# Layer 0's input projection of a two-layer decoder kernel: pairs of column tiles by Strassen's seven products, and mixer outputs kept in DRAM

## The chip, the cores and the metric

The kernel runs on one core of a Trainium2 chip. The metric is the device time of one execution in microseconds (us); of several runs the median is given. Engines are named as in the profile: PE is TensorE's matrix multiplication, PEld its weight loads, DVE is VectorE, ACT is ScalarE, POOL is GpSimd, SP is the engine that issues the DMA transfers here. "L183" is line 183 of the kernel whose trace is read.

## The reference

x has 1024 tokens (SEQ) of 1024 channels (D_MODEL), in float32. Two layers follow each other, then a last RMSNorm. Layer 0, where the change is, computes

```python
def rms_norm(x, g):
    r = x32 * lax.rsqrt(jnp.mean(x32 * x32, axis=-1, keepdims=True) + NORM_EPS)
    return (r * g.astype(jnp.float32)).astype(x.dtype)

def even_mixer(y, w_in, w_pool, pool_scale, conv_w, w_out):
    proj = y @ w_in                       # 1024 x 1024 by 1024 x 6144
    u_a, gate_b, gate_c, h_c, z = jnp.split(proj, [...], axis=-1)
    pooled = causal_multiscale_pool(...)  # trailing means over 2, 4, 8, 16 tokens, minus u_a
    a = jnp.einsum("bsgc,gcd->bsgd", pooled, w_pool).reshape(b, s, POOL_WIDTH) * pool_scale
    cu = gate_c * h_c
    v = conv_w[2] * cu + conv_w[1] * shift_right(cu, 1) + conv_w[0] * shift_right(cu, 2)
    bo = gate_b * v
    out = jnp.concatenate([a, bo], axis=-1) * jax.nn.silu(z)
    return out @ w_out
```

with y the normalized x. Layer 1 is a sliding-window attention with its own projections. The result is 1024 x 1024 in float32.

## The kernel before

**Tiles.** Channels lie on the 128 partitions, tokens along the row, in two halves (HALF) of 512. A column tile of w_in is 128 output channels: 8 contraction tiles of 128x128. w_in has 48 of them: u_a 0 to 7, gate_b 8 to 15, gate_c 16 to 23, h_c 24 to 31, z 32 to 47. Float32 accuracy comes from splitting each operand into a high and a low part (`split`: ACT casts the high part, L175, DVE subtracts it, L176): a product is three matmuls, high·high, high·low and low·high (`mm3`, L182 to L184), each with a 128x128 stationary tile and 512 columns. A column tile costs 8 x 3 matmuls for each half of the tokens (`proj_half`, `proj`).

**The start.** x comes in 16 tiles of 128x512 (`load_x`, L356). ACT multiplies each by g1 into uH (L359), DVE makes the low part uL (L360); no division by the root mean square is made at this point. So the matmuls of the first two column tiles (L411 to L413) take each contraction tile as it arrives. Meanwhile ACT squares x and DVE and POOL add the squares up (L369); column sums by the tensor engine and a Newton iteration (`rsqrt_mean`, L136 to L145) give r for each token, which is spread over all partitions by two matmuls on a diagonal matrix (`diag_r`, L156, and `spread_r`). r enters when a bank of PSUM is emptied, as a factor r_b (L442, L456).

**Order.** TensorE's instructions stand in the order of the program. Those of ACT, DVE and SP stand in program order only in the start (`order()`); from there on a scheduler places them, and an engine takes its instructions strictly in the order placed. Weights are loaded into a pool W of 9 buffers; `take()` splits one unit ahead and loads three ahead. PSUM has banks psA and psD (two each) and psB (four).

**The groups.** Four pooling groups follow (u_a tiles 2g and 2g+1, gates 32+2g and 33+2g, windows 2, 4, 8, 16; the sums over a window are L465 rows of about 1024 columns, and a mixing product with w_pool of 24 matmuls, `mix`), then eight convolution groups (tiles 16+j, 24+j, 40+j, 8+j). The mixer's outputs `o`, 16 x 2 tiles of 128x512, stay in SBUF. The output projection (L564 to L566) takes them, split by `operands(s)`, with w_out. After it comes layer 1.

**Small work.** The rotary tables (`rope_tables`, L203 and further, on DVE) and `small_loads` (the positions posi, the bias bkv and the attention sinks, with nsink on DVE, L248) are placed among the first groups.

## Time and profile before

| | |
|---|---|
| median of three runs | 1156.97 us (1155.9 to 1157.88) |
| span of the profiled execution, its own time from first to last instruction | 1158.2 us |
| PE busy | 1126.6 us, 5248 matmuls |
| DVE, ACT, POOL busy | 619.2, 386.6, 272.6 us |
| mean granted clock of PE | 0.992 |
| bytes moved | 83.92 MB, 72 GB/s over the span |

The span is what the rows of the trace add up to; it is 1.2 us above the median of the other runs. A clock of 1.00 is TensorE's level of 2.4 GHz, 0.5 that of 1.2 GHz. In rows, "x8" is a count of instructions that are run together, "[0.79 <-DVE U L360]" an idle time of the engine just ahead of the row and what ended it.

### The profile page before, as it was taken

The page shows a single profiled execution, that of the slowest core. Times are in us where ns is not written, and L with a number is a line of the kernel's source. Part 1 is how long each engine was busy: PE and PEld are TensorE (multiplying, and loading weights), DVE is VectorE, ACT ScalarE, POOL GpSimd, SP SyncE. Part 2 cuts the span into 40 slices and gives each one's busy share as a digit, 9 for nine tenths or more (in the row PEclk, how much of TensorE's full clock was granted, in tenths as well). Part 3 has the DMA queues.
Part 4 walks back from the last instruction along what each step waited for, and adds up shares of the span by engine and source line. Part 5 has one row for each costly group of instructions (what it writes and reads, how often), then busy time and mean ns, then how long its engine had stood idle before and what let it go on. Part 6 is the DMA issues. An engine that isn't in the chain of part 4 may idle for free.

```text
span 1158.2 us, 14036 instructions
## 1 busy us (share of the span) xinstructions
PE 1126.6 (97%) x5248; PEld 921.5 (80%) x5248; DVE 619.2 (53%) x1109; ACT 386.6 (33%) x797; POOL 272.6 (24%) x427
## 2 busy tenths in 40 slices
PE   9999999999999999999999999999999998898897
PEld 6788888888888888888888788898888886677676
DVE  7993637332233223223655865641133669899995
ACT  8132122111111111111432532420012687776653
POOL 1200000010010110110101100143330036787874
PEclk9899999999999999999999999999999999999999
DMA  7111111111111111111144344520022405460001
GB/s 242 45 47 55 46 52 49 55 41 51 55 37 55 55 37 55 54 38 64 59 148 148 110 164 144 177 80 1 19 69 95 146 19 120 64 90 21 19 19 55
DMA packets 59892, 83.92 MB, mean 72 GB/s; under 512 B 36272, under 2 KB 37424, under 8 KB 59824
## 3 DMA queue, kind: packets, MB, share of 16 engines
q1 hardware_dynamic: 59824, 83.03, 23.4%
q8 instruction: 41, 0.67, 0.2%
q14 instruction: 27, 0.22, 0.1%
HBM read 74.63 MB, written 8.39 MB: 72 GB/s over the span
## 4 chain that ended last, share of the span: by engine, by line
PE 85%; DVE 8%; ACT 3%; issue 1%; DMA 1%; SPq 1%; POOL 0%; ACTq 0%; DVEq 0%
PE psB L184 8%; PE psB L183 8%; PE psB L182 8%; PE psA L184 5%; PE psA L183 5%; PE psA L182 5%; PE psD L184 5%; PE psD L183 5%; PE psD L182 5%; PE psA L566 2%; PE psA L564 2%; PE psA L565 2%; PE psD L566 2%; PE psD L564 2%; PE psD L565 2%
## 5 line engine op out<-in xcount | busy, mean ns | idle before, releaser
L175 ACT CAST W<-W 128x1024 fp32r<-128x1024 f32 (+2 forms) x109 | 107.4, 988 | 531.7 <-DVE W L176 427.0
L176 DVE TENSOR_TENSOR W<-W 128x1024 fp32r<-128x1024 f32 (+2 forms) x109 | 125.4, 1155 | 235.6 <-PE psB L183 177.8
L183 PE MATMUL psB<-U,W 128*128 128x512 f32 x384 | 152.6, 397 | 2.0 <-DVE U L360 1.8
L184 PE MATMUL psB<-U,W 128*128 128x512 f32 x384 | 152.7, 398 | 0.0
L182 PE MATMUL psB<-U,W 128*128 128x512 f32 x384 | 150.7, 392 | 0.0
L183 PEld LDWEIGHTS psB<-U,W 128*128 128x128 f32 x384 | 72.9, 190 | 20.8 <-DVE U L360 4.0
L521 POOL TENSOR_TENSOR T<-T,r_b 128x1024 f32<-128x1024 f32 x8 | 19.3, 2416 | 290.6 <-DVE T L519 290.6
L182 PEld LDWEIGHTS psB<-U,W 128*128 128x128 f32 x384 | 72.9, 190 | 16.4
L184 PEld LDWEIGHTS psB<-U,W 128*128 128x128 f32 x384 | 73.1, 190 | 14.5
L184 PE MATMUL psD<-U,W 128*128 128x512 f32 x184 | 72.5, 394 | 0.0
L184 PE MATMUL psA<-U,W 128*128 128x512 f32 x184 | 72.5, 394 | 0.0
L183 PE MATMUL psD<-U,W 128*128 128x512 f32 x184 | 72.2, 392 | 0.0
L183 PE MATMUL psA<-U,W 128*128 128x512 f32 x184 | 72.1, 392 | 0.0
L182 PE MATMUL psA<-U,W 128*128 128x512 f32 x184 | 71.5, 389 | 0.0
L182 PE MATMUL psD<-U,W 128*128 128x512 f32 x184 | 71.4, 388 | 0.0
L582 POOL TENSOR_TENSOR t<-t,T 128x512 f32<-128x512 f32 x14 | 19.2, 1370 | 170.5 <-ACT T L581 170.5
L734 ACT ACTIVATE pt<-psB,smax 128x128 f32<-128x128 f32 x128 | 45.5, 367 | 25.0 <-DVE smax L731 21.6
L722 PE MATMUL psB<-kT,qT 128*128 128x256 f32 (+1 forms) x128 | 35.2, 297 | 17.3 <-ACT qT L703 9.4
L875 PE MATMUL psD<-O,aH 128*128 128x512 f32 (+1 forms) x128 | 51.1, 399 | 0.0
L566 PE MATMUL psA<-U,W 128*128 128x512 f32 x128 | 50.4, 394 | 0.5 <-DVE W L176 0.5
L566 PE MATMUL psD<-U,W 128*128 128x512 f32 x128 | 50.3, 393 | 0.0
L564 PE MATMUL psD<-U,W 128*128 128x512 f32 x128 | 50.1, 392 | 0.0
(291 smaller groups left out, 2588.0 us busy)
## 6 DMA issues: line engine op xcount, KB each, us to landing
W<-w_in SPq DMA_DIRECT2D x46, 512.0 KB, 3.5
W<-w_out SPq DMA_DIRECT2D x32, 512.0 KB, 3.7
W<-w_z SPq DMA_DIRECT2D x16, 512.0 KB, 3.4
O<-xT SPq DMA_DIRECT2D x16, 256.0 KB, 5.0
T<-xT SPq DMA_DIRECT2D x16, 256.0 KB, 4.2
h_dram<-T SPq DMA_DIRECT2D x16, 256.0 KB, 2.2
W<-w_q SPq DMA_DIRECT2D x8, 512.0 KB, 4.3
U<-h_dram SPq DMA_DIRECT2D x8, 512.0 KB, 5.7
```

The lines of the kernel that those rows point to most:

```text
L175: nc.scalar.copy(out=dst_h, in_=src)
L176: sub(out=dst_l, in0=src, in1=dst_h.bitcast(F32), op=ALU.subtract)
L182: mm(dst, lhsT=ah, rhs=bh, start=(i == 0), stop=False)
L183: mm(dst, lhsT=ah, rhs=bl, start=False, stop=False)
L184: mm(dst, lhsT=al, rhs=bh, start=False, stop=(i == n - 1))
L521: ptt(out=v[:, 0:S], in0=v[:, 0:S], in1=r_b, op=ALU.mult)
L564: mm(dst, lhsT=w[k][0], rhs=oHL[f][0], start=(f == 0), stop=False)
L565: mm(dst, lhsT=w[k][0], rhs=oHL[f][1], start=False, stop=False)
L566: mm(dst, lhsT=w[k][1], rhs=oHL[f][0], start=False, stop=(f == 15))
L722: mm(dst, lhsT=lq, rhs=kT[:, 2 * g, lo:(b + 1) * P], start=True, stop=False)
L734: exps.append(act(out=res[g][:, 2 * i2 + i, :], in_=bv[:, i, P:256], func=AF.Exp, scale=0.125, bias=smax[:, at + i:at + i + 1], accum_out= ...
L875: mm(o, lhsT=a[0][:, kk, :], rhs=woH[8 * n + k][:, c], start=(k == 0), stop=False)
```

## The change

Two column tiles of w_in, 256 output channels, are taken as a matrix of 2 x 2 blocks A (rows: the two column tiles; columns: the two halves of the contraction), and the normalized x as 2 x 2 blocks B (rows: halves of the contraction; columns: halves of the tokens). A block product has four contraction tiles. Instead of eight block products there are seven, of sums of blocks: A11·B11, A12·B21, S1·T1, S2·T2, S3·T3, S4·B22 and A22·T4, where S1 = A21 + A22, S2 = S1 - A11, S3 = A11 - A21, S4 = A12 - S2 and T1 = B12 - B11, T2 = B22 - T1, T3 = B22 - B12, T4 = T2 - B21 up to sign. The sums of weights are made on POOL for each pair (four of 128x512), the sums of x once at the start. Each product is 4 x 3 matmuls (`product`); the partial sums of a pair are combined when its banks are emptied (`pair`: L417, L422, L426, L429, L431 of the new kernel on DVE, a copy L405 on ACT). Three of the seven continue in a bank from which a partial sum has been read, with start=False. LEAD says how many products ahead weights are prepared.

Since the blocks of x are combined across token halves, x is normalized before the first product (`stats`, `normed`, L476, `operand`). The first four products are A11 and A12 of pairs 0 and 1. `spill` writes each finished output to o_dram, and `operands` loads it again. The output projection and layer 1 are the same code.

```diff
...
+    order_ = ("A11", "S2", "A12", "S3", "S1", "A22", "S4")
+    prods = [(0, "A11"), (0, "A12"), (1, "A11"), (1, "A12")]
+    prods += [(i, n) for i in range(2) for n in order_ if n not in ("A11", "A12")]
+    prods += [(i, n) for i in range(2, len(pairs)) for n in order_]
...
+            if what == "S2":
+                wsum[i] = s1 = bp.tile([P, 4, P], F32, name="S1", bufs=2)
+                ptt(out=s1, in0=a21, in1=a22, op=ALU.add)
+                ptt(out=a21, in0=a11, in1=a21, op=ALU.subtract)
+                ptt(out=a11, in0=s1, in1=a11, op=ALU.subtract)
+            if what == "S3":
+                ptt(out=a12, in0=a12, in1=a11, op=ALU.subtract)
...
+            hl = W([P, 2, 4, P], F32R)
+            split(hl[:, 0], hl[:, 1], src)
...
+    def product(dst, i, what, b, start=True):
+
+        prepare_to(at[i, what] + 1 + LEAD)
+        w, x = whl[i, what], ops[b]
+        for k in range(4):
+            for n, (hw, hx) in enumerate(((0, 0), (0, 1), (1, 0))):
+                mm(dst, lhsT=w[:, hw, k], rhs=x[hx][k], start=start and k + n == 0,
+                   stop=k == 3 and n == 2, skip_group_check=not start)
...
+    def pair(i, outs, c11=None, first=None):
+
+        b1, p1 = first or first_products(i)
+        b2 = bank(2)
+        product(b2, i, "S2", "T2")
+        u2_ = t2()
+        tt(out=u2_, in0=b2, in1=p1, op=ALU.add)
+        if first is None:
+            second_products(i, b1)
+            c11(b1)
+        product(b2, i, "S3", "T3", False)
+        tt(out=p1, in0=b2, in1=p1, op=ALU.add)
+        b3 = bank(3)
+        product(b3, i, "S1", "T1")
+        o12, o21, o22 = outs
+        tt(out=o22, in0=b3, in1=p1, op=ALU.add)
+        b4 = bank(4)
+        product(b4, i, "A22", "T4")
+        tt(out=o21, in0=b4, in1=p1, op=ALU.add)
+        product(b3, i, "S4", "B22", False)
+        tt(out=o12, in0=b3, in1=u2_, op=ALU.add)
...
+    def normed(s, r):
+        for k in range(KT):
+            stt(out=xs[s][k], in0=xs[s][k], scalar=col(C_G1, k), in1=r, op0=ALU.mult, op1=ALU.mult)
...
+    load_x(0)
+    load_w(0, 0)
+    load_x(1)
+    load_w(1, 0)
+    load_w(0, 1)
+    r = stats(0)
+    normed(0, r)
+    for k in range(4):
+        operand("B11", k, xs[0][k])
+        operand("B21", k, xs[0][k + 4])
+    r = stats(1)
+    normed(1, r)
+    for k in range(4):
+        b11, b12, b21, b22 = xs[0][k], xs[1][k], xs[0][k + 4], xs[1][k + 4]
+        operand("B22", k, b22)
+        t1 = W([P, 2, HALF])
+        ptt(out=t1[:, 0], in0=b12, in1=b11, op=ALU.subtract)
+        tt(out=t1[:, 1], in0=b22, in1=t1[:, 0], op=ALU.subtract)
+        operand("T2", k, t1[:, 1])
+        operand("T1", k, t1[:, 0])
+        ptt(out=b12, in0=b22, in1=b12, op=ALU.subtract)
+        operand("T3", k, b12)
+        ptt(out=b21, in0=b21, in1=t1[:, 1], op=ALU.subtract)
+        operand("T4", k, b21)
+
+    def spill(f, s, t):
+        nc.sync.dma_start(out=o_dram[f, s], in_=t)
...
                 for i in range(2):
-                    split(h[:, i, :], lo[:, i, :], o[f + i][s])
+                    raw = big2(s)
+                    nc.sync.dma_start(out=raw, in_=o_dram[f + i, s])
+                    split(h[:, i, :], lo[:, i, :], raw)
...
```

What the scheduler and the program order make of it is seen in four places. On TensorE, after the eight matmuls that only warm it up, the kernel before goes straight to the products of the first two column tiles:

```order
L411 MATMUL psD<-U,W 128x512
L412 MATMUL psD<-U,W 128x512
L413 MATMUL psD<-U,W 128x512
L411 MATMUL psA<-U,W 128x512
L412 MATMUL psA<-U,W 128x512
```

In the changed kernel the same place on TensorE has the column sums of both token halves (L464) and the spreading of r (L165), and then the first product A11·B11:

```order
L464 MATMUL b_219<-ones,W 128x2 x32
L165 MATMUL b_289<-W,onesr 128x512 x2
L464 MATMUL b_318<-ones,W 128x2 x32
L165 MATMUL b_388<-W,onesr 128x512 x2
L397 MATMUL b_461<-B11h_149,W 128x512
L397 MATMUL b_461<-B11l_153,W 128x512
L397 MATMUL b_461<-B11h_149,W 128x512
```

All products now stand behind the statistics of both halves. The second place is DVE in the start of the changed kernel, at the end of the preparation of x: B22l, T1l to T4l are low parts of the combined x, L498 makes T2, and "L178 W<-W 128x512 x4" are the low parts of the first four products' weights.

```order
L178 TENSOR_TENSOR B22l_172<-T,B22h_168 128x512
L498 TENSOR_TENSOR W<-T,W 128x512
L178 TENSOR_TENSOR T1l_140<-W,T1h_136 128x512
L178 TENSOR_TENSOR T3l_132<-T,T3h_128 128x512
L178 TENSOR_TENSOR T2l_164<-W,T2h_160 128x512
L178 TENSOR_TENSOR T4l_148<-t_191,T4h_144 128x512
L178 TENSOR_TENSOR W<-W 128x512 x4
L214 TENSOR_SCALAR tr__570<-tr__570 128x64
```

The six rows of this last contraction tile stand ahead of it for the other three too, and before those eight normalizing rows (L476) for each half; the weights of the first products come behind all of them. In the kernel before, DVE had the weights of the first tiles between the tiles of x:

```order
L360 SCALAR_TENSOR_TENSOR U<-O_155,colt,U 128x512
L176 TENSOR_TENSOR W<-W 128x256 x2
L105 CAST identr<-ident 128x128
L360 SCALAR_TENSOR_TENSOR U<-O_172,colt,U 128x512
L360 SCALAR_TENSOR_TENSOR U<-O_182,colt,U 128x512
```

The third place is DVE in the last pooling group of the changed kernel, between the last eviction of the pooled pair (L431) and the third of the gate pair (L426); L519 are window sums, L526 the means, L178 low parts of weights (W) or of pooled values (t), L417 and L422 evictions.

```order
L178 TENSOR_TENSOR W<-W 128x512
L519 TENSOR_TENSOR T<-T 128x1025
L417 TENSOR_TENSOR t_1796<-b_1780,t_1778 128x512
L522 TENSOR_TENSOR T<-T,cinv 128x15
L526 SCALAR_TENSOR_TENSOR T<-T 128x1009
L524 TENSOR_TENSOR T<-T 128x15
L519 TENSOR_TENSOR T<-T 128x1039
L178 TENSOR_TENSOR t_1733<-T,t_1732 128x512
L519 TENSOR_TENSOR T<-T 128x1037
L178 TENSOR_TENSOR t_1737<-T,t_1736 128x512
L519 TENSOR_TENSOR T<-T 128x1033
L422 TENSOR_TENSOR t_1778<-b_1780,t_1778 128x512
```

Ahead of this piece stand, from L431 on, one low part of weights and three L519; behind it, up to L426, one L519, one L526, two small rows and five L178. The evictions of the gate pair now stand among the pooling work of the pair before. The fourth place is SP at the begin of the output projection, where t_4010 and t_4011 are the two halves of the last output tile.

```order
L284 DMA W<-w_out 128x1024 x2
L667 DMA T<-xT 128x512
L284 DMA W<-w_out 128x1024 x3
L507 DMA o_dram<-t_4010 128x512
L507 DMA o_dram<-t_4011 128x512
L655 DMA O_4139<-o_dram 128x512
L655 DMA O_4143<-o_dram 128x512
```

The loads of the output projection's operands stand behind both stores of the last tile; the kernel before has neither.

## Rows read from the trace of the kernel before

**Rows 1.** The page: busy time of the engines, instructions.

```profile
PE 1126.6 (97%) x5248; PEld 921.5 (80%) x5248; DVE 619.2 (53%) x1109; ACT 386.6 (33%) x797; POOL 272.6 (24%) x427
```

**Rows 2.** The page: the chain that ended last, shares of the span by engine.

```profile
PE 85%; DVE 8%; ACT 3%; issue 1%; DMA 1%; SPq 1%; POOL 0%; ACTq 0%; DVEq 0%
```

**Rows 3.** Busy time in stretches: start, layer 0, layer 1.

```profile
core 0: us, PE busy (x) PEld busy (x) DVE busy (x) ACT busy (x) POOL busy (x), PEclk, DMA share, GB/s
10.00:20.00 10.00, 10.00 (x45) 7.91 (x44) 9.38 (x15) 9.82 (x18) 0.00 (x0) 1.00 0.88 299
300.00:400.00 100.00, 100.00 (x438) 82.06 (x437) 27.64 (x31) 13.89 (x15) 10.10 (x8) 1.00 0.14 48
900.00:1000.00 100.00, 93.89 (x508) 76.64 (x507) 77.28 (x171) 72.87 (x202) 44.24 (x50) 1.00 0.33 90
```

**Rows 4.** The instructions of line L564, duration ns, first and last start us.

```profile
L564 PE MATMUL psA<-U,W x128: 388/388/394, 566.4 to 732.2; 128*128 128x512 f32 x128
```

**Rows 5.** The timeline of PE, 30 to 41 us: start, duration, row, idle before.

```profile
30.01 0.69 PE L183 MATMUL psB<-U,W 128*128 128x512 f32 x1 [0.77 <-DVE U L360]
...
34.28 0.77 PE L182 MATMUL psB<-U,W 128*128 128x512 f32 x1
...
39.97 0.59 PE L183 MATMUL psB<-U,W 128*128 128x512 f32 x1
40.40 0.40 PE L184 MATMUL psB<-U,W 128*128 128x512 f32 x1
```

**Rows 6.** The timeline of SP, 19 to 23 us.

```profile
19.67 0.45 SPq L198 DMA_DIRECT2D posi<-pos  x1
...
22.56 0.33 SPq L247 DMA_DIRECT2D sink<-sinks  x1
```

**Rows 7.** DMA issues: KB each, median us to landing.

```profile
W<-w_pool SPq DMA_DIRECT2D x4, 256.0 KB, 2.6
...
sink<-sinks SPq DMA_DIRECT2D x1, 8.0 KB, 4.0
```

**Rows 8.** The timeline of DVE, 22 to 41 us.

```profile
22.59 2.17 DVE L360 SCALAR_TENSOR_TENSOR U<-O,colt,U 128x512 fp32r<-128x512 f32 x3 [0.23 <-ACT U L359]
25.14 6.51 DVE L360 SCALAR_TENSOR_TENSOR U<-O,colt,U 128x512 fp32r<-128x512 f32 x4 [0.38 <-ACT U L359]
...
36.53 0.15 DVE L136 TENSOR_SCALAR rs_v<-psB 128x4 f32<-128x4 f32 x1
...
39.30 0.68 DVE L156 TENSOR_TENSOR W<-ident,rh 128x512 fp32r<-128x512 f32 x1
39.90 0.68 DVE L156 TENSOR_TENSOR W<-ident,rl 128x512 fp32r<-128x512 f32 x1
```

**Rows 9.** The timeline of POOL, 28 to 36 us.

```profile
28.13 7.39 POOL L369 TENSOR_TENSOR t<-t,O 128x512 f32<-128x512 f32 x5 [0.45 <-ACT O L368]
```

**Rows 10.** Instructions grouped by line and form: busy us, mean ns of one.

```profile
L176 DVE TENSOR_TENSOR W<-W 128x512 fp32r<-128x512 f32 x4 | 2.8, 691 | 4.0 <-PE psB L183 3.9
L465 DVE TENSOR_TENSOR T<-T 128x1039 f32<-128x1039 f32 x8 | 9.9, 1237 | 0.3
L369 POOL TENSOR_TENSOR t<-t,O 128x512 f32<-128x512 f32 x7 | 9.7, 1387 | 23.3 <-ACT O L368 23.0
L912 POOL TENSOR_TENSOR U<-U 128x512 f32<-128x512 f32 x15 | 19.3, 1290 | 8.9 <-ACT psD L909 8.9
L175 ACT CAST W<-W 128x512 fp32r<-128x512 f32 x4 | 2.5, 621 | 23.1 <-issue 11.1 <-DVE W L176 7.3 <-PE psB L183 4.7
L377 ACT COPY r_b<-psB 128x512 f32<-128x512 f32 x1 | 0.6, 588 | 5.7 <-PE psB L163 5.7
```

**Rows 11.** Timelines of DVE and POOL beside each other, at 330 and at 703 us.

```profile
330.64 0.68 DVE L442 TENSOR_TENSOR O<-psA,r_b 128x512 f32<-128x512 f32 x1
330.81 2.41 POOL L521 TENSOR_TENSOR T<-T,r_b 128x1024 f32<-128x1024 f32 x1 [34.80 <-DVE T L519]
...
703.55 1.30 POOL L582 TENSOR_TENSOR t<-t,T 128x512 f32<-128x512 f32 x1 [9.68 <-ACT T L581]
703.78 1.35 DVE L583 TENSOR_SCALAR t<-t,colt 128x512 f32<-128x512 f32 x1
```

More of the change, by code (lines that the diff above doesn't have):

```diff
@@ L33 @@
 WARM = 8
-SQ = 6
+W_BUFS = 9
+T3_BUFS = 10
+LEAD = 3
 ZLATE = 6
@@ new lines, in trunk, with first_products @@
+    ops = {}
+    def product(dst, i, what, b, start=True):
[5 more added lines that the diff above has]
+                   stop=k == 3 and n == 2, skip_group_check=not start)
+    def first_products(i):
+        b1 = bank(1)
+        product(b1, i, "A11", "B11")
+        p1 = t2()
+        nc.scalar.copy(out=p1, in_=b1)
+        return b1, p1
@@ new lines, in stats @@
+    def stats(s):
+        acc = bank(3 + s)
+        for k in range(KT):
+            sq = W([P, HALF])
+            act(out=sq, in_=xs[s][k], func=AF.Square)
+            for b in range(4):
+                mm(acc[:, 2 * b:2 * b + 2], lhsT=sq[:, b * P:(b + 1) * P], rhs=ones[:, 0:2],
+                   start=(k == 0 and b == 0), stop=(k == KT - 1), skip_group_check=True)
+        rsqrt_mean(const, rcol0[:, 4 * s:4 * s + 4],
+                   acc[:, 0:8].rearrange("p (b x) -> p b x", x=2)[:, :, 0], 4)
+        dg = diag_r(rcol0, s)
+        bk = spread_r(dg, bank(1 + s))
+        r = W([P, HALF])
+        nc.scalar.copy(out=r, in_=bk)
+        return r
@@ new lines, in half, with silu_, z_pair @@
+    def half(t, s):
+        return t[:, 16 + s * HALF:16 + (s + 1) * HALF]
+    def silu_(dst, src):
+        act(out=dst, in_=src, func=AF.Silu)
+    def z_pair(i, first=None, c11=None):
+        o = [[t3(), t3()], [t3(), t3()]]
+        if c11 is not None:
+            o[0][0] = c11
+        pair(i, (o[0][1], o[1][0], o[1][1]), lambda b1: silu_(o[0][0], b1), first)
+        for d in range(2):
+            for s in range(2):
+                if d or s:
+                    silu_(o[d][s], o[d][s])
+        return o
@@ new lines, in trunk @@
+    f0, f1 = first_products(0), None
+    second_products(0, f0[0])
+    c0 = t3()
+    nc.scalar.copy(out=c0, in_=f0[0])
+    f1 = first_products(1)
+    second_products(1, f1[0])
+    z0 = t3()
+    silu_(z0, f1[0])
+    with tc.tile_pool(name="rope", bufs=1) as pr:
+        rope_tables(pr)
+        small_loads()
+    for g, w in enumerate(WINDOWS):
+        ua = [T(), T()]
+        for t in ua:
+            nc.gpsimd.memset(t[:, 0:16], 0.0)
+        outs = (half(ua[0], 1), half(ua[1], 0), half(ua[1], 1))
+        if g == 0:
+            nc.scalar.copy(out=half(ua[0], 0), in_=c0)
+            pair(0, outs, first=f0)
+        else:
+            pair(2 * g, outs, lambda b1: nc.scalar.copy(out=half(ua[0], 0), in_=b1))
+        pl = [pooled(t, w) for t in ua]
+        o = z_pair(1, f1, z0) if g == 0 else z_pair(2 * g + 1)
+        mix(g, o, pl)
```

334 lines of the change are left out of this document (144 added, 190 removed).

## Prediction

> **What bounds the kernel now.** I read the busy times first, then the chain of waits, then three stretches, then the rows around the start. TensorE is busy 1126.6 us, 97% of the span, VectorE 53% [rows 1], and TensorE holds 85% of the chain that ended last [rows 2]. In the stretch 300 to 400 us, well inside layer 0, TensorE is busy the whole 100 us at a granted clock of 1.00, so its 2.4 GHz level, and issues 438 matmuls: 0.228 us each [rows 3]. There a matmul taken away is time taken away. In 900 to 1000, in layer 1, it is busy for 93.89 us; the change leaves that stage as it was, so all of the effect must appear ahead of layer 0's output projection, or at its begin. The first matmul of that projection (L564) starts at 566.4 [rows 4]. Before it stand 48 column tiles x 8 contraction tiles x 3 products x 2 halves = 2304 matmuls and 4 x 24 of the mixing, 2400 in all; 2400 x 0.228 = 547.2, so the start cost 19.2. The prediction is made for this one mark, 566.4, and carried to the end unchanged.
>
> **What is removed.** 24 pairs of column tiles x 7 products x 12 matmuls = 2016, with the 96 of the mixing 2112: 288 fewer. 2112 x 0.228 = **481.5** for the matmuls alone, 65.7 less. By the Trainium skill's page "TensorE: Matmul & The Clock Gate", section "Wait — 56ns, not 53.3ns?", 512 columns take 215.7 ns from start to start at the fast level; by that the gain would be estimated at 62.1 rather than 65.7, and the 228 ns in the trace of this kernel decides.
>
> **The start.** Before, x enters the products as it arrives, and r is applied later. Now the order on TensorE has both halves' column sums and spreads ahead of the first product, and that product's third matmul needs its weights' low part (the row L178 W<-W x4 on VectorE), which stands behind the whole preparation of x. I follow VectorE's row. (1) Its fourth and ninth rows read posi and sink, which SP issues behind all of x. Before, sink was issued at 22.56 and took 4.0 to land [rows 6, 7]: 26.6. Two weight tiles (1.05 MB) fewer are ahead of it now, at 299 GB/s [rows 3] 3.5: it lands at 23.1. (2) From the first row on the sums to the first diagonal took 2.8 (36.53 to 39.30), the two diagonals 0.60 apart make 1.2 [rows 8]; the spread is two matmuls at 0.43 [rows 5], with an ACT copy of 0.59 [rows 10] and hand-offs 1.8; two weight sums on POOL beside it add 1.2: 30.1. (3) Eight normalizing rows at 0.72 (2.17 for three [rows 8]), eight low parts at 0.61 (the 0.60 between the diagonals [rows 8]), and the second half's 2.8 + 1.2 + 1.8: 46.6. (4) Eight normalizing rows of the second half, each followed by a POOL subtraction that needs it. (5) 24 operand rows and the first of the weights, 25 x 0.61 = 15.3, beside six more POOL instructions.
>
> What (4) and (5) cost depends on whether the two engines hinder each other. In the trace they do: four L360 rows beside POOL took 6.51, 1.63 each, against 0.72 alone, and POOL's five L369 beside them 1.48 each, against 1.29 for an undisturbed addition [rows 8 to 10]. At 703.55 POOL runs 1.30 and VectorE's 128x512 row beside it 1.35, while an eviction from PSUM at 330.64 takes 0.68 beside a POOL row of 2.41 [rows 11]. So I read: rows with all operands in SBUF take turns, evictions do not. Then (4) goes in lockstep, 0.61 + 1.29 = 1.9 for each of eight, 15.2: 61.8; and (5) is 15.3 and six POOL rows of which I take 1.05 of the 1.29, because some fall where VectorE waits anyway: 6.3. The first product can run at **83.4**. If nothing took turns, (4) is 8 x 0.72 = 5.8 and (2) lacks its 1.2: 66.5. Bounds 65 and 89. The Trainium skill's page "SBUF — State Buffer", section "Who interferes with whom", says that a VectorE instruction with two SBUF inputs and a GpSimd one that reads SBUF exclude each other for their whole length. By it the estimate is 66.5 + 14 x 1.29 = 84.6, and the rival without turns would drop out; the trace agrees in the rows named.
>
> TensorE then comes from a pause. Before, after three waits of under 0.8 us and low load the matmuls from 34.28 to 39.97, fourteen, came 0.43 apart, the 1.2 GHz level, not 0.23 [rows 5]: 14 x 0.20 = 2.8 lost. At the first products I take **3** (2 to 4).
>
> **The groups.** Products that accumulate (S3 after S2, S4 after S1, A12 after A11) write a bank that VectorE or ACT must first read. The matmuls between are the cover: 12 x 0.228 = 2.73 for each product. The third of the order pieces shows VectorE in the last pooling group. From the end of the pooled pair (L431) the wait of S4 is for L426. Its cover is six products, 16.4. VectorE has ahead of it and in it two evictions at 0.69, eight L519 rows and two L526 at 1.24 (1.237 measured for the like L465), nine 128x512 rows at 0.61, small rows and L422, L426 themselves: about 21.1 in sum [rows 8, 10]. So TensorE waits 4.7. Counted alike, from L431 to L417: in the second group 11.1 against three products, 8.2: 2.9; in the third 12.7 against 8.2: 4.5; in the first 7.9 against one product (its A12 was done early), 2.7: 5.2. Together 17.3. POOL's weight sums, four of 1.29 a pair, hold VectorE in those stretches; I take 1.7, 2.6, 2.6 and 4.0, which is one to three each: **28.2** (17 to 34). ACT's copies behind the first pairs' products 1.5 and the first pair's own S3 1.2 and the mixing, whose bank has two buffers, 4 x 1.0: **6.7** (3 to 10). Two of the four long waits I let end with the half clock, 2 x 2.8 = **5.6** (0 to 11). The convolution pairs have shorter queues: L431, L607, L610, L612, L417 and two weight rows are 5.7 under a cover of 8.2; three POOL rows in it go over by 1.4 at each of eight places, none by nothing: **3** (0 to 12).
>
> **The transition.** The mixer's output now goes to DRAM and back. On SP the last two stores stand ahead of the first 16 loads (fourth order piece), and the last waits for the last pair's L431, 0.69, and two POOL multiplications, 2.6 [rows 10]. Then an issue of 0.45, a load of 2.6 as for the 256 KB tile w_pool, and a cast of 0.62 [rows 6, 7, 10]: 7.0 in which TensorE has nothing, and after it 2.8 for the half clock: **9.8** (7 to 13). Before, TensorE went on without a wait there. The other transfers lie under the products: 0.26 MB for each tile is little against 299 GB/s, and the DMA engines were busy 14% in 300 to 400 [rows 3].
>
> **Sum.** 83.4 + 481.5 + 3 + 28.2 + 6.7 + 5.6 + 3 + 9.8 = 621.2, against 566.4: 54.8 later. The profiled span was 1158.2, 1.2 above the median of the runs shown, 1156.97. 1158.2 + 54.8 = 1213.0 in the profile's terms, less 1.2: **1212 us**. All low ends give 65 + 481.5 + 2 + 17 + 3 + 0 + 0 + 7 = 575.5, 1166; all high ends 654.5, 1245. Its own range, as not all ends meet, is 1190 to 1235.
>
> **Rivals.** *No taking turns.* If POOL costs VectorE nothing (L369's own mean of 1.39 hardly differs from 1.29 [rows 10], and the slow L360 rows also waited for ACT), the start is 66.5 and the sum 66.5 + 481.5 + 3 + 17.3 + 6.7 + 5.6 + 7.0 = 587.6: 1178. Against it stand the POOL and VectorE rows at 703.55. *The cover holds, the other side.* In the groups VectorE may be ahead of TensorE rather than behind; then no accumulating product waits for its eviction. With the short start this is 66.5 + 481.5 + 3 + 7 = 558.0, 8.4 earlier: 1149, faster. It decides as long as the waits for evictions in all groups stay under 8.4 in total. For it: VectorE is busy only 53% [rows 1], and 16 of 24 pairs have short queues. Against it: the row lengths above, and that it needs the short start too. *The half clock stays.* In a group with many waits TensorE may never regain its fast level: 192 matmuls x 0.20 = 38, less the 2.8 counted: 1247. For it: 30.01 to 40.40 before, where waits of under 1 us sufficed for ten slow us [rows 5]. Against: most of a group is dense. *The reload is the bound.* 16 tiles of 0.26 MB at 299 GB/s are 0.88 each against three matmuls of 0.68: 3.2 more, with another half clock and the weight tiles between them: about 1221. Against: the store's wait is what starts it, and other weights are loaded early.
>
> **How the numbers follow.** Forecast 0.56, no turns 0.17, cover holds 0.15, half clock 0.07, reload 0.05. A measurement of this kernel tells about 0.2%, 2.3 us, from no change. Only the covered case gives faster, and 0.04 of its 0.15 lies within 2.3 us of before: faster 0.11, same 0.04, slower 0.85. The range 1155 to 1250 takes in both cases of turns and the reload and leaves out the covered case below 1155 and half of the slow clock.
>
> **What would show it.** In the new profile: the first product's third matmul near 83, released by VectorE's low part of the weights; VectorE full from about 30 to 83 with rows of 1.2 us or more where POOL is busy; no more than 0.228 us a matmul between waits; TensorE waiting for L417 or L426 once in each pooling group, 3 to 9 us; L426, L417 hardly named in the convolution; one idle time of about 7 us at the first L655 tile; layer 1 as long as before. Wrong would be: the first product by 60 (VectorE's rows shorter than read); the waits in the groups under 8 in total; 512 columns slower than 0.228 us; or a projection that starts near 621 with an end that does not move along.

## The result, and the profile after

The changed kernel takes 1224.34 us (median of four, 1220.65 to 1226.43); the kernel before, run beside it, 1156.43. The ratio is 1.0582, 95% interval [1.0563, 1.0601]: 5.8% slower. The prediction was 1212.

The page of the changed kernel, with the lines that answer to [rows 1, 2], three groups of TensorE's instructions and two of the new DMA issues:

```profile
span 1223.1 us, 14377 instructions
...
PE 1102.5 (90%) x5072; PEld 898.8 (73%) x5072; DVE 763.6 (62%) x1294; ACT 463.2 (38%) x960; POOL 422.2 (35%) x528
...
PE 71%; DVE 19%; ACT 4%; DMA 3%; issue 2%; POOL 1%; SPq 0%; ACTq 0%; DVEq 0%; POOLq 0%
...
L397 PE MATMUL b<-B11h,W 128*128 128x512 f32 x192 | 66.0, 406 | 34.6 <-DVE W L178 26.8
L397 PE MATMUL b<-T3h,W 128*128 128x512 f32 x192 | 68.8, 421 | 21.8 <-DVE t L417 21.8
...
L397 PE MATMUL b<-B22h,W 128*128 128x512 f32 x192 | 65.6, 404 | 7.0 <-DVE t L426 7.0
...
o_dram<-t SPq DMA_DIRECT2D x32, 256.0 KB, 2.0
O<-o_dram SPq DMA_DIRECT2D x32, 256.0 KB, 4.9
```

TensorE is busy 24.1 us less than in [rows 1], not 65.9, in the main since column sums of 27.6 us came in; the rest are slow stretches, below. Its share of the span falls from 97% to 90%, and its share of the chain from 85% to 71%; VectorE's rises from 8% to 19%. The groups name the three places: the first weights (26.8), the third product's eviction L417 (21.8) and the last group's L426 (7.0).

The timeline of TensorE in the changed kernel, the start, one slow stretch, and the first matmuls of the output projection:

```profile
26.54 1.40 PE L165 MATMUL b<-W,onesr 128*128 128x512 f32 x2 [8.12 <-DVE W L158]
29.20 13.81 PE L464 MATMUL b<-ones,W 128*128 128x2 f32 x64 [1.26 <-ACT W L462]
46.68 1.40 PE L165 MATMUL b<-W,onesr 128*128 128x512 f32 x2 [3.67 <-DVE W L158]
55.89 0.80 PE L397 MATMUL b<-B11h,W 128*128 128x512 f32 x1 [7.81 <-ACT W L177]
...
83.88 1.22 PE L397 MATMUL b<-B11h,W 128*128 128x512 f32 x2 [26.78 <-DVE W L178]
...
125.00 0.77 PE L397 MATMUL b<-T3h,W 128*128 128x512 f32 x1 [7.37 <-DVE t L417]
...
618.11 0.39 PE L397 MATMUL b<-B22h,W 128*128 128x512 f32 x1
625.90 0.79 PE L673 MATMUL psD<-U,W 128*128 128x512 f32 x1 [7.40 <-ACT U L177]
```

The first product starts at 55.89 and stops after its second matmul until 83.88. The mark, the first matmul of the output projection, moved from 566.4 [rows 4] to 625.90: 59.5 of the 64.9 us by which the span grew lie ahead of it.

### The profile page after: what moved, and what is told of

Its sections match the earlier page's. It is cut to its first block, busy times and chain, and to the rows that moved or that the text cites. A ratio compares the mean times of both kernels' runs of the same rounds, so it can differ in the third digit from the quotient of the medians.

```text
span 1223.1 us, 14377 instructions
## 1 busy us (share of the span) xinstructions
PE 1102.5 (90%) x5072; PEld 898.8 (73%) x5072; DVE 763.6 (62%) x1294; ACT 463.2 (38%) x960; POOL 422.2 (35%) x528
## 4 chain that ended last, share of the span: by engine, by line
PE 71%; DVE 19%; ACT 4%; DMA 3%; issue 2%; POOL 1%; SPq 0%; ACTq 0%; DVEq 0%; POOLq 0%
PE b L397 35%; PE psA L673 2%; PE psA L674 2%; PE psA L675 2%; PE psD L675 2%; PE psD L674 2%; PE psD L673 2%; DVE T L519 2%; PE psA L184 2%; PE psD L184 2%; PE psA L186 2%; PE psA L185 2%; PE psD L185 2%; PE psD L186 2%; DVE W L178 1%
## 5 line engine op out<-in xcount | busy, mean ns | idle before, releaser
L177 ACT CAST W<-W 128x512 fp32r<-128x512 f32 (+1 forms) x199 | 144.4, 731 | 405.5 <-DVE W L178 122.8
L178 DVE TENSOR_TENSOR W<-W 128x512 fp32r<-128x512 f32 (+1 forms) x199 | 178.6, 903 | 151.9 <-ACT W L177 106.4
L374 POOL TENSOR_TENSOR S<-W 128x512 f32<-128x512 f32 x24 | 33.0, 1377 | 233.5 <-DMA W<-w_in 233.5
L397 PE MATMUL b<-B11h,W 128*128 128x512 f32 x192 | 66.0, 406 | 34.6 <-DVE W L178 26.8
L397 PE MATMUL b<-T3h,W 128*128 128x512 f32 x192 | 68.8, 421 | 21.8 <-DVE t L417 21.8
L397 PE MATMUL b<-B22h,W 128*128 128x512 f32 x192 | 65.6, 404 | 7.0 <-DVE t L426 7.0
L397 PE MATMUL b<-B21h,W 128*128 128x512 f32 x192 | 64.1, 395 | 1.4 <-ACT t L405 1.4
L397 PE MATMUL b<-T1h,W 128*128 128x512 f32 x192 | 63.9, 394 | 0.0
L397 PE MATMUL b<-T4h,W 128*128 128x512 f32 x192 | 63.9, 394 | 0.0
L673 PE MATMUL psD<-U,W 128*128 128x512 f32 x128 | 51.4, 402 | 7.4 <-ACT U L177 7.4
L675 PE MATMUL psD<-U,W 128*128 128x512 f32 x128 | 50.9, 398 | 0.5 <-DVE W L178 0.5
L674 PE MATMUL psD<-U,W 128*128 128x512 f32 x128 | 51.3, 401 | 0.1
L378 POOL TENSOR_TENSOR W<-W 128x512 f32<-128x512 f32 x24 | 31.8, 1325 | 54.2 <-DVE W L178 54.1
L673 PE MATMUL psA<-U,W 128*128 128x512 f32 x128 | 50.4, 394 | 0.0
L674 PE MATMUL psA<-U,W 128*128 128x512 f32 x128 | 50.1, 391 | 0.0
```

Of the source, the lines that this page charges most:

```text
L177: nc.scalar.copy(out=dst_h, in_=src)
L178: sub(out=dst_l, in0=src, in1=dst_h.bitcast(F32), op=ALU.subtract)
L397: mm(dst, lhsT=w[:, hw, k], rhs=x[hx][k], start=start and k + n == 0, stop=k == 3 and n == 2, skip_group_check=not start)
L673: mm(dst, lhsT=w[k][0], rhs=oHL[f][0], start=(f == 0), stop=False)
L674: mm(dst, lhsT=w[k][0], rhs=oHL[f][1], start=False, stop=False)
L675: mm(dst, lhsT=w[k][1], rhs=oHL[f][0], start=False, stop=(f == 15))
```

## The experiments

Twelve kernels. Runs 1 to 9 have one time each, so they tell a difference of about 2.3 us. The theory was that four separate things, all of them order or neighbourhood of rows, cost what the 288 matmuls gave: POOL's sums beside VectorE at the start, the evictions behind pooling work, the transfer ahead of the projection, and the start standing in one line. The main rival was that VectorE simply has too much to do.

**1. The sums of x on VectorE.**

```diff
-        ptt(out=t1[:, 0], in0=b12, in1=b11, op=ALU.subtract)
+        tt(out=t1[:, 0], in0=b12, in1=b11, op=ALU.subtract)
...
-        ptt(out=b12, in0=b22, in1=b12, op=ALU.subtract)
+        tt(out=b12, in0=b22, in1=b12, op=ALU.subtract)
...
-        ptt(out=b21, in0=b21, in1=t1[:, 1], op=ALU.subtract)
+        tt(out=b21, in0=b21, in1=t1[:, 1], op=ALU.subtract)
```

> The three POOL subtractions per contraction tile that combine the blocks of x (L497, L501, L503, twelve in all) are made on DVE instead. Theory (POOL and DVE take turns): DVE has 12 more rows of 0.605 us, but its eight normalizing rows of the second half fall from 11.44 to about 5.4 us and no 1.75 us rows are left there; the third matmul of the first product starts at about 79 (76 to 81) instead of 83.88. Rival (the long DVE rows have another cause, and POOL costs DVE nothing): the 12 rows come on top, the third matmul starts at about 91. Rest of the kernel as before; total about 1219 by the theory, 1231 by the rival.

1218.35, and the third matmul at 76.45 instead of 83.88. VectorE took 12 more rows and was done 7.4 us sooner. The timelines show how; first VectorE and POOL in the changed kernel, second half of the normalization and the operands:

```profile
48.79 11.44 DVE L476 SCALAR_TENSOR_TENSOR T<-T,colt,W 128x512 f32<-128x512 f32 x8
49.69 6.65 POOL L497 TENSOR_TENSOR W<-T,t 128x512 f32<-128x512 f32 x4 [27.15 <-DVE T L476]
...
75.00 0.68 DVE L178 TENSOR_TENSOR T1l<-W,T1h 128x512 fp32r<-128x512 f32 x1
75.60 1.75 DVE L178 TENSOR_TENSOR T3l<-T,T3h 128x512 fp32r<-128x512 f32 x1
...
75.15 1.65 POOL L503 TENSOR_TENSOR t<-t,W 128x512 f32<-128x512 f32 x1 [1.23 <-DVE W L498]
```

Then the same normalizing rows on VectorE in this run:

```profile
49.33 5.39 DVE L476 SCALAR_TENSOR_TENSOR T<-T,colt,W 128x512 f32<-128x512 f32 x8
```

Eight rows take 11.44 beside POOL and 5.39 without it; one low part takes 1.75 beside POOL's L503 and 0.68 next to it. Of the eight, the first two start ahead of POOL's first subtraction and 0.67 apart, the other six run beside it and start 1.67 apart. With eight more such rows among the operands, 14 rows of the start are held, by 1.07 each. So the engines take turns, and POOL pays too (1.65 against 1.29 [rows 10]).

**2. The sums of weights on VectorE.** L374, L375, L376, L378 changed in the same way:

```diff
-                ptt(out=s1, in0=a21, in1=a22, op=ALU.add)
+                tt(out=s1, in0=a21, in1=a22, op=ALU.add)
...
```

> The four sums of weights of each pair (L374, L375, L376, L378) are made on DVE instead of POOL; the start keeps its POOL subtractions. Theory (turns): in the pooling groups each POOL sum held DVE for 1.3 us and is replaced by a DVE row of 0.605; TensorE's waits for L417 and L426 fall from 28.8 to about 21 us (18 to 24), the first product by about 1 us; total about 1215. Rival (no turns): the DVE queues only grow by 0.6 us for each sum, the waits rise to about 34, total about 1231.

1209.40: more than expected, since the start gained 4.7 as well (third matmul at 79.23). POOL's four sums for the first two pairs had held four rows of VectorE there, two among the small rows ahead of the first statistics and two among the operands. TensorE's waits in this run, total, times, longest:

```profile
PE b L397 <- DVE W L178: 24.6, 1, 24.6
PE b L397 <- DVE t L417: 13.9, 4, 6.0
```

In the groups the waits are now 5.97, 2.40, 4.02 and, for a cast of weights in the last, 4.38. Before this edit they were 7.37, 4.59, 6.19 and, in the last group, 1.43 and 7.04.

**3. Pooling behind the gates.** The window sums of a group are emitted after its gate pair, and its mixing one pair later:

```diff
-        pl = [pooled(t, w) for t in ua]
+        if pending:
+            mix(*pending.pop())
         o = z_pair(1, f1, z0) if g == 0 else z_pair(2 * g + 1)
-        mix(g, o, pl)
+        pl = [pooled(t, w) for t in ua]
+        pending.append((g, o, pl))
```

> The same work in another order: in each group the gate pair's evictions are written ahead of the window sums in the program, and the mixing comes one pair later, after the next group's pooled pair; t3 has 12 buffers for it and t2 4. Theory (the waits of TensorE are the order of DVE's queue, not its amount of work): the waits for L417 and L426 fall from 28.8 to under 9 us, with two or three of the half-clock stretches of 2.2 us gone too; the output projection starts at about 600 (596 to 606) instead of 625.9; total about 1198. Rival (DVE has too much work in the groups): TensorE waits elsewhere, at the mixing or in the next pair, the projection starts at 615 or later.

1192.39, 32 us less, by order alone. TensorE's waits for L417:

```profile
PE b L397 <- DVE t L417: 6.6, 2, 5.4
```

That is 1.20 and 5.37, with 1.67 for a row of the last group: 8.2 in all instead of 28.8. The waits of the mixing went from four of 0.84 to three of 0.50. The mark came at 593.4, 32.5 earlier and ahead of what I had expected: 20.6 are these waits, 1.9 the mixing, 6.3 the slow stretches behind three waits that are gone (1.68, 2.33, 2.32), and 3.2 a slower spacing of the matmuls that the changed kernel's profile has there and this one has not (last section).

**4. The last store by POOL's queue; 6. and the loads ahead of the weights.**

```diff
-            spill(f, s, z)
+            if f < 15:
+                spill(f, s, z)
+            else:
+                nc.gpsimd.dma_start(out=o_dram[f, s], in_=z)
```

> The two stores of the last output tile are issued by POOL, which makes the tile, so that on SP the loads of the output projection stand behind no wait for it. Theory (the transition's 7.4 us are the order on SP): the loads of the tiles 0 to 14 are issued several us earlier, TensorE's wait ahead of the projection falls to under 2 us, the half-clock stretch behind it (2.3) goes or shrinks, total 1215 to 1218. Rival (the reload itself is the bound, or the buffers for the loads come free only at the end of the last products): the wait stays at 5 us or more, or comes back in steps between the first matmuls of the projection; total 1222 to 1225.

1218.57; the wait fell from 7.40 to 4.23 only, which lies between the theory (under 2) and its rival (5 or more). The timeline of SP in this run:

```profile
607.48 8.57 SPq L284 DMA_DIRECT2D W<-w_out  x3
616.10 10.97 SPq L658 DMA_DIRECT2D O<-o_dram  x16
```

The loads now stand behind the third weight load, which waits for a buffer W until 616.1. Run 6 puts that load, and the fourth, behind the first 14 loads of o:

```diff
-            nc.sync.dma_start(out=raws[-1], in_=src)
+            if ahead_of and len(raws) > 2:
+                with tc.issue_after(ahead_of[0].ins):
+                    nc.sync.dma_start(out=raws[-1], in_=src)
...
```

> As the fourth experiment, and besides on SP the loads of the output projection's first fourteen tiles stand ahead of its third and fourth weight tile, which waited there until 616 for a buffer. Theory (order on SP, in two places): TensorE's wait ahead of the projection falls from 4.2 to under 1.5 us and the half-clock stretch behind it goes; total 1213 to 1217. Rival (the loads' own buffers come free only with the end of the last pair): the wait stays at 3 us or more, total 1218 or more.

1219.59, no better than run 4 and above what I had expected. TensorE went on without a long wait and no slow stretch follows, but its first matmuls of the projection wait four times, 1.15, 0.72, 0.73 and 1.45. In this run ScalarE casts the loaded tiles without a pause, VectorE makes their low parts behind its last eviction, and POOL still multiplies the last output tile; the last row here is VectorE's first eviction in the projection:

```profile
617.26 8.41 ACT L177 CAST U<-O 128x512 fp32r<-128x512 f32 x16
619.35 4.07 DVE L178 TENSOR_TENSOR U<-O,U 128x512 fp32r<-128x512 f32 x3
619.78 1.40 POOL L624 TENSOR_TENSOR t<-t,T 128x512 f32<-128x512 f32 x1
621.25 1.62 POOL L627 TENSOR_TENSOR t<-t,t 128x512 f32<-128x512 f32 x1
...
633.20 0.69 DVE L690 TENSOR_TENSOR t<-psD,T 128x512 f32<-128x512 f32 x1 [1.95 <-PE psD L684]
```

So the loads had landed; the first three waits are for VectorE's low parts, of which two take 1.77 beside POOL's rows instead of 0.68. The fourth is for the third weight tile's low part: it stands behind L690, which waits 1.95 for TensorE, although ScalarE's cast for it is done at 626.6. Turns and a waiting row again. From the last product of layer 0 to the end of the span the changed kernel takes 605.0, run 4 600.7, run 6 599.6, and before 592.0; so the two edits gained 4.3 and 5.4 at this place.

**5. The start in the order of need.** Both column sums first, then A11 and A12 of the first two pairs, then the second half, with operands T2, T3, T1, T4 in turn, sums on VectorE and the rotary rows at the very begin:

```diff
+    accs = [col_sum(0), col_sum(1)]
+    rs = [stats(0, accs[0]), stats(1, accs[1])]
+    normed(0, rs[0])
...
+    f0, f1 = first_products(0), None
+    second_products(0, f0[0])
...
+    normed(1, rs[1])
...
```

> Only the start is reordered, with the sums of x on DVE as in the first experiment: the column sums of both halves stand ahead of both spreads on TensorE; the products A11 and A12 of pairs 0 and 1 stand, in the program, ahead of the second half's normalization, so that DVE makes B11, B21 and their weights first; the operands of x follow in the order T2, T3, T1, T4; the rotary tables are made at the very begin (positions loaded ahead of x), while DVE waits for x. Theory (the start's price is what stands ahead of the first product, 66.9 us more than the 17.0 of before): the third matmul of the first product starts at about 34 (32 to 38) instead of 83.88, S2 of pair 0 at about 57 instead of 98.5, its S3 at about 66 instead of 103.6, and the output projection 36 to 42 us earlier than 622 (625.9 without the 3.3 us in which that one execution ran 1.9% slow), at 580 to 586; total 1181 to 1188. Rival (the amount of DVE's work before the first pair can end is what counts, not its order): pair 0 still ends after 100, projection at 610 or later, total above 1208.

1210.59, a miss; here is TensorE in this run:

```profile
7.37 25.76 PE L467 MATMUL b<-ones,W 128*128 128x2 f32 x120 [0.79 <-ACT W L465]
...
49.66 1.22 PE L397 MATMUL b<-B11h,W 128*128 128x512 f32 x2 [2.54 <-DVE W L178]
...
86.67 0.79 PE L397 MATMUL b<-T3h,W 128*128 128x512 f32 x1 [7.21 <-DVE t L417]
```

Two things were overlooked. The column sums hold TensorE to 33; and L417, which empties the bank that the third kind of product needs, stood on VectorE behind the rows that make T4. The total is what the rival had (above 1208); the mark, at 608.5, lies between the theory's 580 to 586 and the rival's 610.

**7. The edits of 5, 3 and 6 together; 8. and 2.** No new lines.

> The three changes of order together: the start of the fifth, the groups of the third, the transition of the sixth experiment. Theory (three separate losses that add): 67.9 us slower than before, minus 38 (start), minus 32 (groups), minus 9 (transition): about 1146 (1140 to 1155), so a little faster than the kernel before at 1157. Rival (the losses share a cause, DVE's load, and one returns where another is taken away): 1165 or more.

1172.87, a time that I had given to the rival (1165 or more). Its reason does not hold, though: from 1224.34 the three edits took 13.8, 32.0 and 4.8 by themselves, 50.5 in sum; together 51.5. The parts add up, and none returned; I had set the start's part too high.

> As the seventh, with the four sums of weights of each pair on DVE as in the second experiment. Theory (turns cost DVE 1.3 us for each POOL sum in the pooling groups, a DVE row costs 0.605): 3 to 8 us less than the seventh, about 1141. Rival (with the new order POOL's sums fall where DVE has slack): equal within 2 us, or slower by up to 4 as DVE's queues grow.

1157.69, 15.2 less, about twice what was expected at the most, where run 2 by itself gave 14.9. The product of the third kind came at 81.95 instead of 86.73, its next wait fell from 5.38 to 1.11, and a last one of 1.67 went. This is level with the kernel before (1156.44, run beside it).

**9. Cheap column sums; 10. with all of 8.** The squares are added first, half 0 on VectorE, half 1 on POOL, so that a half needs four column-sum matmuls instead of 32; the rotary rows go to the convolution:

```diff
+        for k in range(1, KT):
+            more = W([P, HALF])
+            act(out=more, in_=xs[s][k], func=AF.Square)
+            (tt, ptt)[s](out=sq, in0=sq, in1=more, op=ALU.add)
...
```

> The fifth experiment again, after its miss, with what its trace showed taken away: the squares of a half are added up first (DVE for half 0, POOL for half 1) and only the sum goes through TensorE, 4 matmuls of 2 columns for each half instead of 32, which had taken 0.2 us and twice each; the rotary tables move from the start into the second convolution group; T1 and T4 are made behind pair 0's first eviction (L417) instead of ahead of it. Theory (the fifth missed because the column sums held TensorE until 33 us and L417 stood behind the rows of T4): third matmul of the first product at 33 to 37 instead of 49.66, S3 of pair 0 at 58 to 64 instead of 86.67, projection 22 to 28 us earlier than 608.5; total 1183 to 1190. Rival (DVE's amount of work): S3 of pair 0 not before 75, total above 1198.

1212.81, and the third kind came at 80.83: what the rival had given, but not by its reason. TensorE waited 21.44 for POOL's last addition, until 40.98. POOL's additions stood behind two weight sums that waited 17.92 for their transfer, and behind squares that ScalarE had behind a copy that waited 7.81 for TensorE; and one addition was held for 5.93 by rows of VectorE (last section).

> The eighth experiment (all orders, sums of weights on DVE) with the start of the ninth. Theory: another 18 to 24 us less than the eighth's 1157.7, about 1136 (1132 to 1141), a ratio of 0.979 to 0.987 to the kernel before. Rival (without POOL's turns the start gains less, and DVE's 14 more rows in each group of pairs make new waits): 1147 or more.

1166.79, a ratio of 1.0084 [1.0070, 1.0098] to before; a miss, 9 us slower than run 8. The timelines of VectorE and ScalarE in run 10:

```profile
19.87 0.69 DVE L378 TENSOR_TENSOR S<-W 128x512 f32<-128x512 f32 x1 [9.85 <-DMA W<-w_in]
...
29.81 0.58 ACT L483 COPY W<-b 128x512 f32<-128x512 f32 x1 [18.52 <-PE b L165]
```

The scheduler set a weight sum that waits for its transfer ahead of the last additions of squares, and a copy that waits for TensorE ahead of the second half's squares. What stood behind could have run. So the theory became: it is not how much there is, but that a waiting row at the head of an engine's queue holds the ready ones.

**11. The start written by hand.** From run 8, ScalarE, VectorE and SP in the order of the program until pair 0 ends, squares added on VectorE, each normalized row followed by what it feeds:

```diff
+    ordered.enter_context(tc.manual_schedule(
+        engines={mybir.EngineType.Activation, mybir.EngineType.DVE, mybir.EngineType.SP}))
...
+    for k in range(KT):
+        norm1(0, k, r0)
+        nc.scalar.copy(out=ops["B11" if k < 4 else "B21"][0][k % 4], in_=xs[0][k])
...
```

> The kernel of the eighth run (every order changed, both operands' sums on VectorE; 1157.69 us, first product of the third kind at 81.95) with the rows of the start written out by hand for ScalarE, VectorE and the transfer queue until the first pair ends: squares added on VectorE, four column-sum matmuls in each half, each normalized row followed by the operand rows that it feeds, the rotary rows and small loads behind pair 0. No row then stands ahead of one that is ready before it, which is what held the run before it up. If the start is bound by the order of the rows, the first product comes at 33 to 38, that of the third kind at 55 to 62, and the whole at 1132 to 1140 (1157.7 less 20 to 25). If the amount of VectorE's rows at the start decides (the sums, the squares' additions and the weights' sums are now all its own), the product of the third kind comes at 75 or later and the whole is 1150 or more.

The first product came at 32.59, as expected, the third kind only at 74.88, and the time was 1159.78, ratio 1.0019 [1.0009, 1.0029]: as VectorE's amount would have it. The timelines of TensorE and VectorE in this run speak against that reason:

```profile
42.24 0.50 PE L401 MATMUL b<-B11h,W 128*128 128x512 f32 x1 [1.19 <-ACT W L177]
...
59.67 0.79 PE L401 MATMUL b<-T2h,W 128*128 128x512 f32 x1 [9.66 <-ACT W L177]
...
42.22 0.69 DVE L178 TENSOR_TENSOR W<-W 128x512 fp32r<-128x512 f32 x1 [5.46 <-ACT W L177]
46.70 0.69 DVE L178 TENSOR_TENSOR W<-W 128x512 fp32r<-128x512 f32 x1 [3.79 <-ACT W L177]
```

VectorE, supposedly the one with too much to do, idled for 5.46 and then 3.79: my own order had the casts of pair 1's weights on ScalarE behind copies that wait for TensorE, and the weight sums for the second kind of product behind the first two contraction tiles of T2, ten rows, until 55.82.

**12. No row that waits ahead of one that is ready.** These casts go ahead of the copies, the sums into the hole, each low half some rows behind its cast:

```diff
+        if hold[0]:
+            late.append(lambda: tt(out=dst_l, in0=src, in1=dst_h.bitcast(F32), op=ALU.subtract))
+            return None
...
-    r1 = r_row(spread(1))
+    b1_ = spread(1)
+    hold[0] = True
+    prepare_to(4)
+    r1 = r_row(b1_)
...
+    prepare_to(5)
+    flush(1)
     f1 = first_products(1)
...
```

> The start by hand of the eleventh run (1159.78 us; first product 32.59, second kind 59.67, third kind 74.88), with the rows put so that no engine's queue holds one that waits while ready ones stand behind it: ScalarE's casts of pair 1's weights ahead of the copies that wait for TensorE, the pair's weight sums in the hole of VectorE between 36.8 and 42.2, every low half some rows behind its cast, and no row of pair 1's sums ahead of pair 0's rows. If rows that wait at the head of a queue were what held the eleventh run, the first product stays at 32 to 34, the second kind comes at 46 to 51, the third at 57 to 63, the mark at 541 to 548 and the whole at 1139 to 1147. If VectorE's amount decides (its rows from 36.8 on add up to what it needs anyway), the third kind comes at 70 or later and the whole stays at 1154 or more.

1142.12, ratio **0.9861 [0.9841, 0.9881]**: 1.4% faster than the kernel before, and within all that was expected (the second kind started at 49.2). The page of run 12, and TensorE's timeline:

```profile
PE 1068.9 (94%) x4960; PEld 869.8 (76%) x4960; DVE 786.6 (69%) x1416; ACT 461.5 (40%) x960; POOL 259.6 (23%) x422
...
PE 75%; DVE 17%; ACT 4%; issue 2%; DMA 1%; POOL 0%; SPq 0%; DVEq 0%; ACTq 0%
```

```profile
12.86 1.84 PE L489 MATMUL b<-ones,W 128*128 128x2 f32 x8 [8.01 <-DVE W L484]
...
32.87 0.63 PE L413 MATMUL b<-B11h,W 128*128 128x512 f32 x1
...
60.81 0.76 PE L413 MATMUL b<-T3h,W 128*128 128x512 f32 x1 [2.65 <-DVE t L434]
...
543.77 0.50 PE L819 MATMUL psD<-U,W 128*128 128x512 f32 x1 [1.16 <-DVE U L188]
```

VectorE is busier than in the changed kernel (786.6 against 763.6), and the whole is 82 us shorter. So the rival, VectorE's amount, falls for the whole way from 1224 to 1142. Not all of that way is order: the column sums fell from 27.6 to 3.7 us of TensorE, and POOL's sums moved. The 17.7 from run 11 to run 12 are order alone. What is left at the start can be amount: from 42.3 to 60.7 VectorE idles for less than 0.5 us in all. The mark, taken as the matmul behind the first wait, is 543.8 (one matmul ran alone at 542.2). With 2112 x 0.2289 = 483.4 for the matmuls, the start and all waits cost 60.4; before they cost 566.4 - 2400 x 0.2289 = 17.0. Of the 65.9 that the 288 matmuls give, 43 still go there: no product can start before x is normalized (32.87; before, x entered as it arrived), and the first ones do not run on.

## Why the prediction was right, point by point

Slower, with all of the four costs where they were put. The terms, in us, up to the mark:

| term | predicted | measured |
|---|---|---|
| third matmul of the first product | 83.4 | 83.88 |
| 2112 matmuls | 481.5 | 483.4, by 0.2289 each |
| half clock at the first products | 3 | 2.0 (to 87.89) |
| waits for L417 and L426 in the groups | 28.2 | 26.6, the first pair's S3 apart |
| copies, first S3, mixing | 6.7 | 7.0 (1.4, 2.2, 3.4) |
| half clock in the groups | 5.6 | 8.6, four stretches |
| convolution | 3 | 0 |
| transition | 7.0 + 2.8 | 7.4; its slow stretch of 2.8 lies behind the mark |
| sum | 621.2, so 618.4 up to the mark | 618.9 of 625.9 |

*The matmuls.* 0.2289 from start to start, where the prediction divided 100 us by the 438 records of [rows 3]. The 215.7 ns of the Trainium skill's page "TensorE: Matmul & The Clock Gate", section "Wait — 56ns, not 53.3ns?", are not seen in this kernel. Of the 7.0 that the table leaves, 3.2 are a slower spacing from 450 us on in this one execution, below; the other 3.8 lie, roughly, in small pieces at the edges of the waits, of the slow stretches and between banks. "512 columns slower than 0.228 us" was a sign of being wrong that the prediction named itself: for some 720 matmuls it came true, at 0.2333.

*The start.* The end was right, and by luck, since its steps were off both ways. In step (1) and (2) VectorE's first row on the sums was at 22.92 (23.1 predicted), but not for the sink: VectorE waited for the positions, as its row in the changed kernel shows,

```profile
20.08 1.14 DVE L202 CAST posf<-posi 128x8 f32<-128x8 int32 x1 [17.76 <-DMA posi<-pos]
```

and then took 2.84 for that row and the eight behind it, two of them held by POOL's weight sums; the sink's own row, at 23.22, did not wait. The first normalizing row came at 28.65, not 30.1. Step (3) left out TensorE: the column sums of the second half, 13.81 us, held it until 43.0, VectorE waited 4.19 for them, and the second half's normalization began at 48.79 instead of 46.6. Step (4) was too dear: the eight rows took 11.44, not 15.2, since two of them ran before POOL had anything to subtract and the other six took 1.67 a turn, not 1.90. Step (5) went from 60.2 to 83.9, 23.7 against 21.6: eight rows were held in it and not six, two of them by weight sums that the prediction had not put there. The errors of +2.2, -3.8 and +2.1 nearly cancel. The mechanism, turns, is what run 1 shows, and the rival without turns is out. The rule of the Trainium skill's page "SBUF — State Buffer", section "Who interferes with whom", that such rows exclude each other, agrees with 0.68 against 1.75. The estimate of 84.6 that the prediction worked out from it is as near as 83.4 is, but by other parts: it counted 14 turns of 1.29, and the trace has 14 held rows by 1.07 each. The VectorE row at 703.78, which the prediction read as such a turn, is no instance of two operands in SBUF: L583 reads one tile and a column. It takes 0.49 at its shortest and 1.35 there, so rows with one tile are held too; the cast of the positions above is another, 1.14 beside POOL and 0.17 in run 2, where POOL has no sum there.

*The groups.* Counted without POOL the prediction had 5.2, 2.9, 4.5 and 4.7; run 2, whose sums are not POOL's, has 5.97, 2.40, 4.02 and 4.38, the last by another releaser. For POOL it added 10.9 in all; the difference between the two kernels is 9.8. Run 3 shows the mechanism: the same rows in another order, and the waits fall to 8.2. The rival of a cover that holds needed less than 8.4 in total and the short start; neither was there. In the convolution the shorter queues cost nothing.

*The half clock.* Every wait of 4.59 or more in the groups was followed by a stretch of 3.8 to 5.1 us at the 1.2 GHz spacing that cost 1.7 to 2.3, so four in the groups and not two; after each the matmuls came 0.23 apart again, so the rival in which the fast level never returns is out.

*The transition.* 7.4 against 7.0, by the steps named. SP, ScalarE in the changed kernel:

```profile
618.74 3.53 SPq L507 DMA_DIRECT2D o_dram<-t  x2
...
622.32 4.92 SPq L655 DMA_DIRECT2D O<-o_dram  x10
...
625.23 1.31 ACT L177 CAST U<-O 128x512 fp32r<-128x512 f32 x2 [5.65 <-DMA O<-o_dram]
```

The second store's issue ends at 622.27, the first load comes right behind it, the cast 2.9 after that. The rival in which the reload is the bound is out for the changed kernel, and no run shows it as what comes next: in run 6 the loads had landed, and the waits that are left are for VectorE's low parts.

*What was wrong: the end does not move along.* Behind the mark the changed kernel takes 597.2, before 591.8 [rows 4, and the span]: 5.4 that the prediction had at nothing, and one of the signs that it named itself. The last line of the output projection, before and in the changed kernel (first and last start):

```profile
L566 PE MATMUL psD<-U,W x128: 392/394/398, 577.9 to 743.6; 128*128 128x512 f32 x128
...
L675 PE MATMUL psA<-U,W x128: 388/390/398, 640.5 to 806.3; 128*128 128x512 f32 x128
```

From the mark to the last of these starts it is 177.2 before and 180.4 in the changed kernel, 3.2 more. Of them 2.8 are the slow stretch behind the mark (625.9 to 631.5), which the prediction had counted in its transition. The other 2.2 lie in layer 1, whose code is the same but whose rows the scheduler placed anew: from the projection's end to the end of the span it is 414.6 before, 416.8 here, and between 415 and 419 in the twelve runs. Their cause stays open. In run 12, which has no slow stretch there, the part behind the mark is 597.9, with waits of 0.72, 0.73 and 1.46 at its begin; they are for VectorE's low parts, as in run 6.

The 1212 is 12 below the 1224.34: 7.5 at the mark (625.9 against the 618.4 without the slow stretch), 2.6 behind it, which is the 5.4 less that stretch, and 2.4 in that this profile's span lies 1.2 below its median where that of before lies 1.2 above the median shown.

## What to carry to other kernels

Fewer multiplications are worth their full 0.229 us each only where nothing new stands ahead of them: first write down which rows of the other engines must be done before the first product and before each bank is written again, in the order in which each queue holds them. When such a change turns out slower, try the order before the amount: here moving rows and sums, and cheaper column sums, gave back 82 us while VectorE's work grew. Parts that end in different waits add up (13.8, 32.0, 4.8 and 14.9 by themselves, 65.4 in sum, and 66.7 together), so they can be measured one by one.

## What the runs showed that I had not expected

- A column sum by float32 matmuls with two columns is not small. The 64 rows of the program show as 128 records, 64 in 13.81: 27.6 us of TensorE at the start, as much as 121 matmuls of 512 columns. Run 1 has the same sums at two speeds, here in windows of its L464 (behind the window stand its length, busy time and records of TensorE, those of its weight loads, and the granted clock):

```profile
5.00:8.00 3.00, 2.09 (x20) 2.00 (x19) 1.00 0.87 263
9.00:18.00 9.00, 8.69 (x40) 8.61 (x40) 0.50 1.04 399
```

  That is 0.10 for a record at 1.00, the 2.4 GHz level, and 0.22 at 0.50, that of 1.2 GHz. In the changed kernel nearly all come at the slow spacing, 0.213 apart, though the granted clock of its profile reads 1.00 there. So by run 1 about half of the 27.6 would be the clock, which is likely and not shown. With the squares added first, eight records are left in each half, 1.84 us (run 12).
- From 450.8 to 617.9 us of the changed kernel's profiled execution the matmuls came 0.2333 apart instead of 0.2289, without a wait, 1.9% more; runs 1 to 4 and 12 have 0.229 there. Shorter stretches of it stand in runs 5, 7 and 9, at other times. Its cause is open.
- Turns need not be one for one. In run 9 an addition of POOL was held for 5.93 while VectorE put eight low parts through at their usual 0.60; undisturbed such an addition takes 1.29 [rows 10]:

```profile
29.63 5.93 POOL L466 TENSOR_TENSOR W<-W 128x512 f32<-128x512 f32 x1 [2.54 <-ACT W L465]
...
29.55 2.48 DVE L178 TENSOR_TENSOR B11l<-t,B11h 128x512 fp32r<-128x512 f32 x4
31.95 2.49 DVE L178 TENSOR_TENSOR B21l<-t,B21h 128x512 fp32r<-128x512 f32 x4
```

- What a wait costs behind it is not told by its length alone. Waits of 1.2 to 1.4 us in dense work were followed by no slow matmuls (runs 6 and 12). One of 2.65 after a thin stretch was followed by 13 of them from 60.81 on, 2.4 us in all (run 12); there the granted clock was at 0.50 from 54.9 on, ahead of that wait, while the products waited for their operands by 0.6 to 1.3 each. After a wait of 2.19 in the changed kernel (103.61) the matmuls came 0.23 apart at once; after one of 2.16 in run 10 (341.42) ten came 0.40 apart.
